# A bank's sigmoid and second product one bank later; the output projection's first two token tiles in two halves over four PSUM banks

## Chip, cores and metric

The kernel runs on one core of one Trainium2 chip. The metric is the device time of one execution in microseconds; lower is better.

## What is computed

A two-layer encoder trunk on 512 tokens of width 1024, all in float32. Per layer (cut to what matters here):

```python
proj = rms_norm(h) @ w_in                       # 1024 -> 9 groups of 512 columns
rq, rk, rv, rg, hq, hf_fwd, hf_bwd, hi, hg = split(proj)
q2 = silu(hq) * 128 ** -0.5                     # HGRN2 query
k  = (1 - lb) * sigmoid(-hf);  f = lb + (1 - lb) * sigmoid(hf)   # two directions; lb = 0 in layer 0
r_out = rms_normalize(retention(rotary(rq), rotary(rk), rv)) * ret_g * silu(rg)
h_out = rms_norm(hgrn2(q2, k, f, hi)) * hgrn_g * silu(hg)
h = h + concat([r_out, h_out]) @ w_out          # 1024 -> 1024
h = h + expert_choice_ffn(rms_norm(h))          # 16 SwiGLU experts, 64 tokens each
```

A final RMSNorm ends it.

## The kernel before, in words

**Order.** `body` runs, for each of the two layers, `mixer` (projections, both recurrences, output projection, router) and then `ffn` (the experts in eight pairs). The program order is written out by hand: every engine takes its instructions in the order in which the Python code emits them, and waits in that order. "Below" names lines of `before.py`.

**Memory.** SBUF has 22 slots of 1 MB, handed out first in, first out by `slot` and returned by `put`. Weights come through one queue, SP's, in the order of `plan` (`pump`, L179). A load into a slot waits until the slot's last reader is done, and the loads behind it wait too. PSUM has eight banks: four with the tag `pj` for the projections and the experts' gate and up products, four with the tag `pb` for all else.

**Precision.** An fp32 product is made of three passes: the operands are split into a high part (fp32r, by ScalarE: L448, L819, L808) and a low part (the rest, by VectorE or GpSimd: L449, L820, L809), and high by high, low by high and high by low are summed in PSUM.

**Projections.** `proj` (L475) makes one group of 512 columns in four banks, one for each 128 columns, in four steps q of 24 matmuls of 128x512; each step takes a quarter of the contraction. In the last step bank c is complete after each six matmuls, and `evacuate(c, ...)` follows at once. The next group takes the same four banks in the same order, so its first matmul into bank c waits for the evacuation of that bank. `split` makes the parts of the step after next's weights and stands in the queues behind the evacuations. The groups run in the order hq, hf_bwd, hf_fwd, hi, rq, rk, rv, rg, hg (n = 0 to 8).

**Evacuations.** `silu_q` (L500 to L502), `forget` (L487 to L493), `gate_out` (L515 to L517) and `mix_out` (L801 to L809) each run all their steps for one bank before the next bank's. VectorE multiplies the bank by the row of 1/rms (`rb`), which frees the bank; ScalarE takes the sigmoid; VectorE waits for it and makes the second product (in `forget` two products with the lower bound, in layer 1 only). In `mix_out` there follow a product with the recurrence's output and the split of the previous bank's result into high and low parts; the last bank's own split comes at its end.

**Side work.** `lead` runs a projection and, each six matmuls, takes some steps of a side generator: in projection 0 `arrive` (transposes of h, their split, the squares, 1/rms, and four small matmuls that spread it over the partitions, L416), in 3 to 7 the recurrences, in 8 `norms` and half of the split of `w_out` (`wout_split`).

**Output projection.** `output` (L925) goes through eight (token tile, half of the columns) pairs. Each takes one `pj` bank, and 24 matmuls: eight contraction tiles k in three passes. k = 0 to 3 are the retention heads, ready during projection 8; k = 4 to 7 are the HGRN2 heads, which `mix_out` delivers at its end. The sum with h (L935), the transposes (L954), the router (L986 to L1017) and the search for each expert's best tokens (L1042) follow as `work`.

**Layer boundary.** The last pair of experts is added to h in column pieces of 512, 256 and 256. The last piece's sums (`last_spread`, L1223 and L1228) are made in layer 1's `arrive`, one bank for each of four token tiles.

## Time and profile before

| | |
|---|---|
| median of three runs | 1668.72 us (1667.14 to 1672.53) |
| the profiled execution | 1667.63 us, of which the span from first to last instruction is 1665.9 us |
| busy PE / VectorE / ScalarE / GpSimd | 1555.7 / 680.3 / 478.4 / 237.4 us |
| mean granted TensorE clock | 0.979 |
| read from HBM | 459.03 MB |

Times in the trace are microseconds from the span's start. PE is TensorE, DVE VectorE, ACT ScalarE, POOL GpSimd; L475 is line 475. In the timeline a line gives start, duration, engine, line, instruction, output and input, the shapes and the count; in square brackets stands the time for which the engine was idle ahead of it, and which instruction released it. The mixer of layer 0 takes the first 385 us, its experts go on to about 835 us; layer 1's mixer ends at about 1208 us.

### The profile page before, as it was taken

The numbers are of one execution on the slowest core, as the hardware profiler recorded it, in microseconds if no ns is written. First come the engines' busy times: TensorE is split into PE (matmuls) and PEld (weight loads), VectorE is DVE, ScalarE is ACT, GpSimd is POOL, SyncE is SP. The second block draws the span as 40 slices with busy tenths as digits, with TensorE's granted clock in tenths as the row PEclk, the third lists the DMA queues.
The fourth block names the chain that finished last, engine by engine and source line by source line (L and its number), as shares of the span: only waits on it lengthen the run. The fifth ranks groups of instructions, "written<-read, shape, count | busy, mean of one in ns | idle before, by whom it ended". The sixth has DMA issues, their size and how long they took to land. (4 is left out here: it accounts for less than half of the span.)

```text
span 1665.9 us, 20044 instructions
## 1 busy us (share of the span) xinstructions
PE 1555.7 (93%) x8020; PEld 965.8 (58%) x8020; DVE 680.3 (41%) x1123; ACT 478.4 (29%) x888; POOL 237.4 (14%) x208
## 2 busy tenths in 40 slices
PE   7989899899999999999999898998899999999986
PEld 6778797675454444433477687976653545444333
DVE  4477955652111312312254889465610213132113
ACT  4444344352130110200243344444422212012003
POOL 1042542200000000011000534421000000000201
PEclk9999999899999999999999899998999999999998
DMA  6120221649999999999950111316689999999997
GB/s 254 53 76 26 76 97 52 250 157 358 426 417 427 426 427 425 427 426 427 401 213 26 51 51 51 122 51 227 268 350 426 424 426 427 427 427 426 426 426 277
DMA packets 94605, 464.53 MB, mean 279 GB/s; under 512 B 7904, under 2 KB 16288, under 8 KB 48432
## 3 DMA queue, kind: packets, MB, share of 16 engines
q1 hardware_dynamic: 93040, 458.35, 67.6%
q0 software_dynamic: 1472, 4.90, 0.8%
q8 instruction: 63, 1.03, 0.2%
q14 instruction: 30, 0.25, 0.0%
HBM read 459.03 MB, written 4.19 MB: 278 GB/s over the span
## 5 line engine op out<-in xcount | busy, mean ns | idle before, releaser
L1168 PE MATMUL pj<-s,s 128*64 128x512 f32 x2048 | 476.1, 596 | 18.0 <-DMA s<-in_w_up_dram 14.7
L475 PE MATMUL pj<-s,s 128*128 128x512 f32 x1728 | 435.6, 405 | 19.7 <-DVE s L449 8.8
L475 PEld LDWEIGHTS pj<-s,s 128*128 128x128 f32 x1728 | 325.6, 193 | 92.2 <-DVE s L449 11.6
L1168 PEld LDWEIGHTS pj<-s,s 128*64 128x64 f32 x2048 | 171.8, 137 | 279.7 <-issue 205.8
L1301 PE MATMUL pb<-s,t 128*64 128x512 f32 x896 | 197.5, 594 | 5.4 <-ACT t L1206 2.7
L1301 PEld LDWEIGHTS pb<-s,t 128*64 128x64 f32 x896 | 65.0, 137 | 127.5 <-issue 113.3
L1085 POOL TENSOR_TENSOR t<-s,t 128x512 fp32r<-128x512 f32 x16 | 20.9, 1327 | 714.8 <-ACT t L1083 714.8
L1216 DVE SCALAR_TENSOR_TENSOR t<-pb,sm,t 128x512 fp32r<-128x512 f32 (+1 forms) x34 | 24.4, 719 | 240.3 <-ACT t L1215 238.8
L1228 DVE TENSOR_TENSOR s<-s,pb 128x512 f32<-128x512 f32 (+1 forms) x116 | 68.7, 653 | 129.7 <-PE pb L1223 129.7
L925 PE MATMUL pj<-s,s 128*128 128x512 f32 x384 | 105.4, 422 | 10.0 <-ACT s L808 6.7
L449 DVE TENSOR_TENSOR s<-s,s 128x1024 fp32r<-128x1024 f32 (+1 forms) x64 | 82.4, 1306 | 28.8 <-ACT s L448 28.5
L925 PEld LDWEIGHTS pj<-s,s 128*128 128x128 f32 x384 | 72.8, 199 | 32.0 <-ACT s L808 9.2
L1133 DVE COPY sm<-pb 128x2 f32<-128x2 f32 x16 | 2.5, 159 | 203.3 <-PE pb L1130 203.3
L1215 ACT ACTIVATE t<-pb,sm 128x512 fp32r<-128x512 f32 (+1 forms) x34 | 22.5, 662 | 194.4 <-PE pb L1301 182.9
L1111 PEld LDWEIGHTS pb<-t,t 128*128 128x128 f32 x512 | 66.0, 203 | 14.0 <-issue 9.7
L448 ACT ACTIVATE s<-s 128x1024 fp32r<-128x1024 f32 (+1 forms) x73 | 73.9, 1035 | 0.1
L1144 ACT ACTIVATE t<-pb 128x512 fp32r<-128x512 f32 x16 | 9.6, 601 | 220.6 <-PE pb L1142 220.6
L1111 PE MATMUL pb<-t,t 128*128 128x256 f32 x512 | 70.5, 296 | 1.6 <-DVE t L1095 0.8
L1223 PE MATMUL pb<-t,t 128*128 128x512 f32 (+1 forms) x264 | 68.0, 398 | 1.0 <-DVE s L1228 0.9
L1223 PEld LDWEIGHTS pb<-t,t 128*128 128x128 f32 x264 | 45.8, 188 | 34.3 <-issue 19.4
L568 DVE TENSOR_TENSOR s<-s,s 128x512 f32<-128x512 f32 x56 | 57.4, 1026 | 13.2 <-PE pb L616 13.2
L1189 ACT ACTIVATE t<-pj,sm 128x512 f32<-128x512 f32 x32 | 22.0, 687 | 140.2 <-PE pj L1168 140.2
(234 smaller groups left out, 1602.7 us busy)
## 6 DMA issues: line engine op xcount, KB each, us to landing
s<-in_w_gate_dram SPq DMA_DIRECT2D x124, 1024.0 KB, 19.5
s<-in_w_up_dram SPq DMA_DIRECT2D x124, 1024.0 KB, 19.5
s<-in_w_down_dram SPq DMA_DIRECT2D x112, 1024.0 KB, 19.5
s<-in_w_in_dram SPq DMA_DIRECT2D x34, 1024.0 KB, 4.8
s<-in_w_down_dram SPq DMA_DIRECT2D x32, 512.0 KB, 10.4
s<-in_w_out_dram SPq DMA_DIRECT2D x8, 1024.0 KB, 4.8
s<-in_x_dram SPq DMA_DIRECT2D x8, 512.0 KB, 3.7
s<-in_w_gate_dram SPq DMA_DIRECT2D x8, 512.0 KB, 11.1
```

What stands on the lines that cost most here:

```text
L448: nc.scalar.activation(wh[:, ks], src[:, ks], AF.Copy)
L449: e.tensor_tensor(low[:, ks], src[:, ks], wh[:, ks], op=OP.subtract)
L475: nc.tensor.matmul(pg[c], lhsT=lhsT, rhs=rhs, start=(k == 0 and m == 0), stop=(k == ND - 1 and m == 2))
L568: v.tensor_tensor(qv, qv, tq, op=OP.mult)
L925: nc.tensor.matmul(po, lhsT=x, rhs=w, start=(k == 0 and i == 0), stop=(k == ND - 1 and i == 2))
L1111: nc.tensor.matmul(pt[:, i], lhsT=x[:, tt, k % 2::2], rhs=oh[:, tt], start=(tt == 0 and x is self.picked[u][0]), stop=(tt == NT - 1 and x ...
L1168: nc.tensor.matmul(pg[n + 2 * f][e * CAP:(e + 1) * CAP], lhsT=self.xe[:, k, at + e * CAP:at + (e + 1) * CAP], rhs=w[e][:, f * 512:(f + 1) ...
L1215: nc.scalar.activation(yH[0][:, cs], py, AF.Copy, scale=gate)
L1216: v.scalar_tensor_tensor(yL[0][:, cs], py, gate, yH[0][:, cs], op0=OP.mult, op1=OP.subtract)
L1223: nc.tensor.matmul(pc, lhsT=ohT[:, tt * P:(tt + 1) * P], rhs=y[:, cs], start=(y is yH[0]), stop=(y is yL[0]))
L1228: v.tensor_tensor(dst, dst, pc, op=OP.add)
L1301: nc.tensor.matmul(py[f][e * CAP:(e + 1) * CAP], lhsT=hT[:, k, e * CAP:(e + 1) * CAP], rhs=W[e][:, k2, f * 512:(f + 1) * 512], start=(k == ...
```

## The change

- `forget`, `silu_q`, `gate_out` and `mix_out` do the product that frees the bank (`scaled`) and the sigmoid at once. The rest is put into a queue (`follow`), which first runs one round of what earlier banks left (`flush(1)`). So a bank's second product stands behind the next bank's first. In `mix_out` the low part lags by one more bank. The last bank's rest is run by `lead` at its second to eleventh step, or by `flush()` at the end of projection 8.
- `output` takes the first two token tiles as four banks: first k = 0 to 3 for all four, then k = 4 to 7. `plan` and `wout_split` take `w_out` with the retention half first.
- `arrive`: 1/rms is spread two steps (twelve matmuls) later; in layer 1 the last piece's squares move ahead of the transposes of k = 4 to 7, and `last_spread` takes two token tiles to a bank.
- The scaling of the rotary table moves from the end of projection 0 to the end of projection 1.
- At the start the gain's transpose stands behind two token tiles, not three; the second half of the first weight's low part goes to GpSimd.

```diff
@@ start
-        self.turn_in(range(4), range(NT - 1))
+        self.turn_in(range(4), range(2))
         self.norm_gain()
-        self.turn_in(range(4), range(NT - 1, NT))
+        self.turn_in(range(4), range(2, NT))
@@ arrive
             self.last_squares(1)
             yield 1.0
+            self.last_squares(2)
...
         for _ in self.rstd_steps(0, NT, self.r):
             yield 1.0
+        yield 1.0
+        yield 1.0
         yield 1.0
@@ split
+                if ks.start:
+                    e = nc.gpsimd
@@ new helpers
+    def scaled(self, dst, ps):
+        self.nc.vector.tensor_tensor(dst, ps, self.rb, op=OP.mult)
+        return dst
+    def follow(self, *steps):
+        self.flush(1)
+        self.second.append(deque(steps))
+    def flush(self, rounds=9):
+        for _ in range(rounds):
+            for d in list(self.second):
+                d.popleft()()
+                if not d:
+                    self.second.remove(d)
@@ forget
-        nc.vector.tensor_tensor(F, ps, self.rb, op=OP.mult)
+        self.scaled(F, ps)
...
-            nc.vector.tensor_scalar(F, F, om, lb, op0=OP.mult, op1=OP.add)
-            nc.vector.tensor_scalar(K, K, om, None, op0=OP.mult)
+            def bound():
+                nc.vector.tensor_scalar(F, F, om, lb, op0=OP.mult, op1=OP.add)
+                nc.vector.tensor_scalar(K, K, om, None, op0=OP.mult)
+            self.follow(bound)
@@ silu_q (gate_out alike)
-        nc.vector.tensor_tensor(q, ps, self.rb, op=OP.mult)
-        nc.scalar.activation(sg, q, AF.Sigmoid)
-        nc.vector.scalar_tensor_tensor(q, q, P ** -0.5, sg, op0=OP.mult, op1=OP.mult)
+        nc.scalar.activation(sg, self.scaled(q, ps), AF.Sigmoid)
+        self.follow(lambda: nc.vector.scalar_tensor_tensor(q, q, P ** -0.5, sg, op0=OP.mult, op1=OP.mult))
@@ mix_out
+        nc.scalar.activation(sg, self.scaled(w, ps), AF.Sigmoid)
+        def mix():
+            v.scalar_tensor_tensor(w, w, g, sg, op0=OP.mult, op1=OP.mult)
+            v.tensor_tensor(o, o, w, op=OP.mult)
+            for H, _, x in self.mixed(NH + c, o):
+                nc.scalar.activation(H, x, AF.Copy)
+        def low():
+            for H, L, x in self.mixed(NH + c, o):
+                v.tensor_tensor(L, x, H, op=OP.subtract)
+        self.follow(mix, low)
@@ lead
+            n += 1
+            if 1 < n < 12:
+                self.flush(1)
@@ output
-        for tt, f in [(tt, f) for tt in range(NT) for f in range(2)]:
+        both, po = [(tt, f) for tt in range(2) for f in range(2)], {}
+        parts = [(tt, f, range(a, a + 4)) for a in (0, 4) for tt, f in both] + \
+            [(tt, f, range(ND)) for tt in range(2, NT) for f in range(2)]
+        for tt, f, ks in parts:
...
+            if ks[-1] < ND - 1:
+                continue
@@ last_spread
-                self.last_spread = lambda: [spread(tt, lo, n) for tt in range(NT)]
+                def last_spread():
+                    for t in range(0, NT, 2):
+                        pc = self.pb().rearrange("p (t c) -> p t c", t=2)
+                        for tt in (t, t + 1):
+                            for y in yH[0], yL[0]:
+                                nc.tensor.matmul(pc[:, tt - t], ...)
+                        h = self.h[t // 2][:, :, lo:]
+                        v.tensor_tensor(h, h, pc, op=OP.add)
```

## The prediction

> **What bounds the kernel now.** I read the slices of the page first, then the table by stage, the chain, and the timeline of the two mixers.

> ```profile
> DMA  6120221649999999999950111316689999999997
> ```
> ```profile
> 500.00:520.00 20.00, 20.00 (x94) 1.00 1.01 426
> ```
> ```profile
> 1607.86 20.83 DMA s<-in_w_up_dram
> ```
> ```profile
> 1158.00:1161.00 3.00, 3.00 (x29) 1.00 0.02 8
> ```

> The slices (41.6 us each) alternate: in both expert stages the DMA engines are full, 426 GB/s in the stage table, and the chain there runs through weight loads of some 20 us each. In the mixers they are nearly empty. So the experts are paced by their weight stream, and the mixers by TensorE and what it waits for. A saving in a mixer reaches the end only if the stream starts earlier by as much. It does: in the output projection the DMA share is 0.02, because all slots are taken; they come free as this projection's tiles and then the first experts' weights are used up, which is tied to TensorE's place. I therefore count every microsecond that a mixer loses less as one microsecond of the end. Next, where TensorE waits.

> **The output projection.** Timeline of layer 1, then the clock there, then layer 0:

> ```profile
> 1122.83 11.08 PE L475 MATMUL pj<-s,s 128*128 128x512 f32 x48
> ...
> 1133.37 0.68 DVE L801 TENSOR_TENSOR t<-pj,s 128x512 f32<-128x512 f32 x1
> ...
> 1134.10 3.02 PE L925 MATMUL pj<-s,s 128*128 128x512 f32 x12 [0.19 <-DVE t L801]
> ...
> 1134.75 0.75 DVE L803 SCALAR_TENSOR_TENSOR t<-t,cols,t 128x512 f32<-128x512 f32 x1 [0.70 <-ACT t L802]
> ...
> 1135.53 0.69 DVE L804 TENSOR_TENSOR s<-s,t 128x512 f32<-128x512 f32 x1
> ...
> 1136.14 0.68 DVE L801 TENSOR_TENSOR t<-pj,s 128x512 f32<-128x512 f32 x1
> ...
> 1137.85 0.73 PE L925 MATMUL pj<-s,s 128*128 128x512 f32 x2 [0.73 <-ACT s L808]
> ...
> 1145.92 1.42 DVE L809 TENSOR_TENSOR s<-s,s 128x256 fp32r<-128x256 f32 x4
> ```
> ```profile
> 1151.15 5.71 PE L925 MATMUL pj<-s,s 128*128 128x512 f32 x24
> ```
> ```profile
> 1143.00:1146.00 3.00, 1.83 (x3) 0.50 0.86 311
> ```
> ```profile
> 310.97 3.01 PE L925 MATMUL pj<-s,s 128*128 128x512 f32 x12 [0.18 <-DVE t L801]
> ...
> 328.24 2.09 PE L925 MATMUL pj<-s,s 128*128 128x512 f32 x8
> ```

> Undisturbed, a matmul costs 11.08 / 48 = 0.231 us. The first pair does its twelve retention matmuls and then waits, head by head, for `mix_out`, whose banks follow each other by about 2.8 us (1133.37, 1136.14); the wait quoted (0.73 us) is the first of a row of them that lasts until the last low part (1145.92 to 1147.34). The granted clock falls to 0.50 on the way. From 1134.10 to 1151.15 TensorE does 30 matmuls (and four transposes, 0.4 us in steady state): 17.05 us for 30 x 0.231 + 0.4 = 7.3 us of work.

> After the change there are 48 retention matmuls to do first, 11.1 us, to about 1145.2. They need a free bank each 2.8 us: VectorE frees the four at 1134.0, 1134.6, 1136.8 and 1139.6 if I lay its queue out with the durations of before (0.68 for a first product, 0.75 + 0.69 for the two behind it, 1.42 / 2 = 0.7 for a low part), so each is in time. The last low part is then due at about 1145.4; the first bank gets to that head after another nine matmuls, at 1147.3. Even with `mix_out` as slow as now (1147.34) the cover holds. Gain 17.05 - 7.3 = 9.8 us in layer 1, and by the same count 328.24 - 310.97 - 7.3 = 10.0 us in layer 0. If only the waits go and the half clock stays, some 2.3 us less (half of a stretch of 3 us, the one quoted, to 6 us), about 7.5 us each. The sums with h come a few matmuls later for tile 0, but both tiles are complete after the same 96 matmuls as before, so router and search keep their places.

> **Projection 0 to 1, layer 0.**

> ```profile
> 44.29 0.68 DVE L500 TENSOR_TENSOR s<-pj,s 128x512 f32<-128x512 f32 x1
> ...
> 46.34 1.22 DVE L847 TENSOR_TENSOR t<-t,s 128x1024 f32<-128x1024 f32 x1
> ...
> 48.26 3.89 ACT L448 ACTIVATE s<-s 128x1024 fp32r<-128x1024 f32 x4
> ...
> 49.35 0.50 PE L475 MATMUL pj<-s,s 128*128 128x512 f32 x1 [2.47 <-ACT s L448]
> ...
> 50.80 50.85 PE L475 MATMUL pj<-s,s 128*128 128x512 f32 x215 [0.95 <-DVE s L449]
> ```
> ```profile
> 52.00:55.00 3.00, 3.00 (x8) 0.50 0.99 354
> ```

> The last bank's first product starts only at 44.29, because each bank waits for the sigmoid of the one before. Behind it stand the rotary table (1.22 us), the lower bound and the next weights' split; TensorE waits 2.47 + 0.95 us and then runs at half clock for some 3 us. With the lag the last first product moves to about 41.6 and the table goes away, so the weights' low part is ready at about 46.7, when TensorE gets there (46.88, the end of its 24 matmuls). 216 matmuls from 46.88 at 0.231 end at 96.8 in place of 101.65: 4.9 us. Bounds: 2.5 (some of the wait and of the slow clock stays) and 5.4.

> **The two starts.**

> ```profile
> 31.52 1.13 PE L416 MATMUL pb<-ident,sm 128*128 128x128 f32 x8 [0.71 <-DVE sm L332]
> ```
> ```profile
> 834.61 0.50 PE L1223 MATMUL pb<-t,t 128*128 128x256 f32 x2 [0.95 <-DVE s L1228]
> ...
> 851.40 1.13 PE L416 MATMUL pb<-ident,sm 128*128 128x128 f32 x8 [1.67 <-DVE sm L332]
> ```

> Twelve more matmuls (2.8 us) ahead of L416 cover its waits of 0.71 and 1.67 us, and 1/rms is still on its way 1.4 us before the first bank is complete. Two banks in place of four take away 0.95 us. Together 0.7 in layer 0 and 2.6 in layer 1 (bounds 1.5 and 2.9). The squares moved ahead on ScalarE delay the split of k = 4 by about 0.6 us, and TensorE needs that only two steps later. The other order at the very start and the half on GpSimd are worth nothing that I can see, 0 to 0.3 us: projection 0 reaches that low part after twenty matmuls.

> **The forget gates, layer 1** (layer 0 has no second product there):

> ```profile
> 867.24 20.56 PE L475 MATMUL pj<-s,s 128*128 128x512 f32 x89 [0.85 <-DVE s L449]
> ...
> 892.58 20.59 PE L475 MATMUL pj<-s,s 128*128 128x512 f32 x89 [0.76 <-DVE s L449]
> ```
> ```profile
> 904.96 0.69 DVE L487 TENSOR_TENSOR s<-pj,s 128x512 f32<-128x512 f32 x1 [9.04 <-PE pj L475]
> ...
> 913.68 0.68 DVE L487 TENSOR_TENSOR s<-pj,s 128x512 f32<-128x512 f32 x1
> ...
> 914.42 1.66 PE L475 MATMUL pj<-s,s 128*128 128x512 f32 x6 [1.25 <-DVE s L487]
> ...
> 915.60 1.04 ACT L448 ACTIVATE s<-s 128x1024 fp32r<-128x1024 f32 x1
> ...
> 916.73 3.27 POOL L449 TENSOR_TENSOR s<-s,s 128x1024 fp32r<-128x1024 f32 x1 [79.77 <-DVE s L493]
> ...
> 920.06 8.00 PE L475 MATMUL pj<-s,s 128*128 128x512 f32 x23 [2.86 <-POOL s L449]
> ```
> ```profile
> 936.96 3.97 PE L475 MATMUL pj<-s,s 128*128 128x512 f32 x12
> ```
> ```profile
> 86.55 0.69 DVE L487 TENSOR_TENSOR s<-pj,s 128x512 f32<-128x512 f32 x1 [10.04 <-PE pj L475]
> ...
> 93.69 2.39 POOL L449 TENSOR_TENSOR s<-s,s 128x1024 fp32r<-128x1024 f32 x1 [48.83 <-ACT s L448]
> ```
> ```profile
> 113.56 3.00 PE L475 MATMUL pj<-s,s 128*128 128x512 f32 x12
> ```

> A bank takes (913.68 - 904.96) / 3 = 2.9 us here and TensorE fills one in 6 x 0.231 = 1.4, so the next group waits for bank 3, and then for its weights, whose split stands behind. With the lag the four first products follow TensorE and end about 4 us earlier. At 0 to 1 the 0.85 us goes. At 1 to 2, 96 matmuls take 25.34 us (867.24 to 892.58) for 22.2: 3.2 us (bounds 2 and 3.3). At 2 to 3 GpSimd's split and the recurrence's first steps on GpSimd and VectorE set the pace afterwards, so I don't take the waits but layer 0 as the measure, where no second product stands in the way: from the first evacuation to the same group of twelve it needs 113.56 - 86.55 = 27.0 us, layer 1 936.96 - 904.96 = 32.0. With about 1 us for the two bounds that stay on VectorE: 4.0 us, bounds 1 and 5.3.

> **The retention gate** (L516 and L517 before the head norms):

> ```profile
> 291.24 0.49 PE L714 MATMUL pb<-t,selR 128*128 128x512 f32 x1 [1.07 <-ACT t L704]
> ```
> ```profile
> 1114.37 0.49 PE L714 MATMUL pb<-t,selR 128*128 128x512 f32 x1 [1.78 <-ACT t L704]
> ```

> The sigmoids end about 1.5 us earlier, but the last bank's product (0.75 us) now falls into the chain of the norms. I take 0.3 and 1.0 us, bounds -0.8 and 1.8 for each.

> **Sum.** Layer 0: 0.7 + 4.9 + 0.3 + 10.0 = 15.9. Layer 1: 2.6 + 0.9 + 3.2 + 4.0 + 1.0 + 9.8 = 21.5. Together 37.4 us: 1667.63 - 37.4 = 1630.2 us, by the profiled execution, which lies 1.1 us under the median of the three runs. I put the forecast at 1630.5.

> **Rivals.** *The lag does little.* Only the four banks and the starts work (19.8 + 3.3), since behind each bank some other queue is due at once. For it: at 920.06 the wait names GpSimd. Against it: the wait of 2.47 us at 49.35 goes back to VectorE's order. About 1644.5; chance 0.07.

> *Four banks cost the clock.* The 48 matmuls go through four banks; if that kept the granted clock at 0.50 in both layers, they would take 11.1 us more each: 1652.7. Against it stands 1122.83: the projections go through four banks too, at 0.231. Chance 0.02. [...]

> *The stream hides it.* If the experts' loads were fixed by something other than TensorE's place, the mixers' gain would be waited away: 1667.6, no change. Against it stands the empty DMA at 1158. Chance 0.03.

> *VectorE and GpSimd get in each other's way, and it is slower.* The same GpSimd split takes 2.39 us at 93.69 and 3.27 us at 916.73, where VectorE works beside it: 0.9 us more. The change lays 64 lagged VectorE instructions (24 in layer 0, 40 in layer 1) beside GpSimd's splits and recurrence steps. If each cost 0.9 us on the path, 58 us against 37: about 1688. It decides from 42 of them on; most lie where GpSimd is idle. Chance 0.02. [...]

> *It does not do what it says*: `flush` would have to stand ahead of the next bank's first product in VectorE's queue. In the diff `scaled` comes first everywhere, so I leave that inside the first rival.

> **Chances.** Forecast 0.86, the rivals as given. Faster by over 0.3% (5 us, about what can be told here) 0.95, the same 0.03, slower 0.02. The range: the lower bounds of the terms add up to some 21 us, the upper ones to 41; with the first rival inside and a few microseconds for a stage that runs on at full clock, 1622 to 1646.

> **What would show it.** Right: L925 in one run of 48 matmuls of about 11 us in each layer with no wait for L808 or L809; granted clock 1.00 there; no wait of L475 for L487; projection 1 of layer 0 without a wait for the weights' split; no wait ahead of L416. The mixers 16 and 21 us shorter, the expert stages as long as now. Wrong: waits in the second half of the four banks, expert stages that grow by what the mixers lose, or longer GpSimd instructions at the recurrence's start.

## The result and the profile after

The changed kernel takes 1630.76 us (median of four runs, 1630.17 to 1632.15), the kernel before 1667.93 us beside it (four runs, 1666.37 to 1672.53): a ratio of 0.9774, interval 0.9753 to 0.9795. The profiled execution took 1630.17 us (span 1628.4, mean granted clock 0.986), 37.46 us less than the one of before.

TensorE's way through the two mixers, in spans between first matmuls of a kind, in us:

| stretch | layer 0 before | after | layer 1 before | after |
|---|---|---|---|---|
| start of the span or of the expert stage to first projection matmul | 12.85 | 11.26 | 442.03 | 441.01 |
| projections 0 to 2, to the recurrence's first parity sum | 89.09 | 84.13 | 96.57 | 82.88 |
| parity sums, to the first level (L616, now L640) | 10.49 | 10.33 | 7.54 | 10.51 |
| to the first head norm row (L714, now L738) | 178.81 | 178.22 | 178.94 | 178.86 |
| to the first output matmul (L925, now L961) | 19.73 | 19.72 | 19.73 | 19.73 |
| output projection and router, to the first gather (L1111, now L1149) | 74.64 | 65.13 | 74.11 | 65.12 |
| to the first expert matmul | 3.68 | 3.39 | 3.44 | 3.54 |
| last experts, to the end | | | 454.25 | 454.57 |

The rows add up to the span. Up to its first expert, layer 0 is 17.1 us shorter, layer 1's mixer 19.7, the first expert stage 1.0, and the last expert stage is 0.3 longer: 37.5 us less. So what TensorE no longer waits for reaches the end, and the expert stages keep their length. The page after, its DMA slices and the table by stage for one of them:

```profile
DMA  6121121668999999999950121217799999999997
```
```profile
500.00:520.00 20.00, 19.85 (x106) 10.15 (x104) 5.46 (x9) 2.57 (x4) 0.00 (x0) 1.00 1.01 426
```

The full slices are as many as before and the stream runs at the same 426 GB/s. That it begins earlier shows in the table: layer 0's first expert matmul stands at 372.18 us in place of 389.29.

**Output projection.** Timeline of TensorE, layer 0 and layer 1 of the kernel after, and VectorE beside layer 1:

```profile
303.66 14.59 PE L961 MATMUL pj<-s,s 128*128 128x512 f32 x63 [0.19 <-DVE t L489]
...
1105.17 14.57 PE L961 MATMUL pj<-s,s 128*128 128x512 f32 x63 [0.18 <-DVE t L489]
...
1104.44 1.27 DVE L489 TENSOR_TENSOR t<-pj,s 128x512 f32<-128x512 f32 x2
...
1107.21 0.68 DVE L489 TENSOR_TENSOR t<-pj,s 128x512 f32<-128x512 f32 x1
...
1109.87 0.68 DVE L489 TENSOR_TENSOR t<-pj,s 128x512 f32<-128x512 f32 x1
...
1115.73 0.76 DVE L835 TENSOR_TENSOR s<-s,s 128x256 fp32r<-128x256 f32 x2 [0.48 <-ACT s L831]
```

The 63 matmuls of the first two token tiles up to the first transpose run without a wait, 14.57 / 63 = 0.231 us each. The four banks come free 0.1 us before the first output matmul (the second 0.5, the third 2.7 and the fourth 5.4 after it), and the last low part (L835) ends 11.3 us after it. The first bank gets to that head only after 57 matmuls, 13.2 us. The table of windows for that stretch of layer 1, before and after:

```profile
1134.00:1151.00 17.00, 12.09 (x33) 7.55 (x34) 10.99 (x21) 5.81 (x14) 0.00 (x0) 0.70 0.94 337
```
```profile
1105.17:1119.74 14.57, 14.57 (x63) 11.75 (x63) 10.75 (x20) 5.25 (x12) 0.00 (x0) 1.00 0.98 338
```

In the first row TensorE does 33 matmuls (30 of the output, the rest transposes) in 17 us at a mean clock of 0.70, in the second 63 in 14.6 us at 1.00. VectorE does 21 and 20 instructions of nearly the same total (10.99 and 10.75 us): it is no faster, only in another order.

**Projections, layer 0 and layer 1.** TensorE's timeline of the kernel after:

```profile
32.18 1.05 PE L418 MATMUL pb<-ident,sm 128*128 128x128 f32 x8
...
45.90 49.20 PE L479 MATMUL pj<-s,s 128*128 128x512 f32 x215 [0.90 <-DVE s L453]
...
832.97 1.05 PE L418 MATMUL pb<-ident,sm 128*128 128x128 f32 x8
833.78 54.91 PE L479 MATMUL pj<-s,s 128*128 128x512 f32 x241
890.27 5.51 PE L479 MATMUL pj<-s,s 128*128 128x512 f32 x23 [1.59 <-POOL s L453]
896.07 0.73 PE L627 MATMUL pb<-s,parity 128*128 128x512 f32 x2 [0.28 <-ACT s L618]
899.16 0.73 PE L627 MATMUL pb<-s,parity 128*128 128x512 f32 x2 [2.35 <-POOL s L619]
...
902.57 2.50 PE L479 MATMUL pj<-s,s 128*128 128x512 f32 x5 [2.46 <-DVE s L453]
```

The last row's counterpart before:

```profile
931.10 1.45 PE L475 MATMUL pj<-s,s 128*128 128x512 f32 x5 [0.22 <-DVE s L449]
```

The spread of 1/rms (L418) waits for nothing. In layer 0 the wait of 2.47 us for ScalarE is gone and 0.90 of the 0.95 us for the low part is left. In layer 1 one run of 241 matmuls (0.228 us each) stands where before six waits cut it, and of the wait of 2.86 us for GpSimd's split 1.59 is left. Then come the parity sums, where TensorE waits for GpSimd (L619, 2.35 us) and for a low part of VectorE (2.46 us, before 0.22): this stretch of layer 1 is 3.0 us longer than before (the last section).

**Head norms.** The kernel after, the row before the norms and their first row:

```profile
1070.62 8.49 PE L479 MATMUL pj<-s,s 128*128 128x512 f32 x29 [1.79 <-DVE s L453]
...
1085.44 0.49 PE L738 MATMUL pb<-t,selR 128*128 128x512 f32 x1 [0.79 <-ACT t L728]
```

The wait at the norms fell from 1.78 to 0.79 us. The row above it took 8.49 us for its 29 matmuls; what that means follows below.

### The profile page after: what moved, and what is told of

Same layout as the page of the kernel before. It is cut to its first block, busy times and chain, and to the rows that moved or that the text cites. A ratio compares the mean times of both kernels' runs of the same rounds, so it can differ in the third digit from the quotient of the medians.

```text
span 1628.4 us, 20039 instructions
## 1 busy us (share of the span) xinstructions
PE 1543.3 (95%) x8020; PEld 960.0 (59%) x8020; DVE 675.3 (41%) x1120; ACT 478.2 (29%) x888; POOL 237.5 (15%) x209
## 5 line engine op out<-in xcount | busy, mean ns | idle before, releaser
L479 PE MATMUL pj<-s,s 128*128 128x512 f32 x1728 | 432.7, 403 | 11.3 <-DVE s L453 8.9
L453 DVE TENSOR_TENSOR s<-s,s 128x1024 fp32r<-128x1024 f32 (+1 forms) x63 | 84.2, 1351 | 35.9 <-ACT s L450 35.7
L961 PE MATMUL pj<-s,s 128*128 128x512 f32 x384 | 95.1, 398 | 0.4 <-DVE t L489 0.4
L961 PEld LDWEIGHTS pj<-s,s 128*128 128x128 f32 x384 | 69.8, 189 | 15.9 <-DVE t L489 1.2
L1149 PEld LDWEIGHTS pb<-t,t 128*128 128x128 f32 x512 | 65.9, 203 | 14.2 <-issue 9.7
L1149 PE MATMUL pb<-t,t 128*128 128x256 f32 x512 | 70.3, 296 | 2.1 <-DVE t L1133 1.3
```

Of the source, the lines that this page charges most:

```text
L453: e.tensor_tensor(low[:, ks], src[:, ks], wh[:, ks], op=OP.subtract)
L479: nc.tensor.matmul(pg[c], lhsT=lhsT, rhs=rhs, start=(k == 0 and m == 0), stop=(k == ND - 1 and m == 2))
L961: nc.tensor.matmul(po[tt, f], lhsT=x, rhs=w, start=(k == 0 and i == 0), stop=(k == ND - 1 and i == 2))
L1149: nc.tensor.matmul(pt[:, i], lhsT=x[:, tt, k % 2::2], rhs=oh[:, tt], start=(tt == 0 and x is self.picked[u][0]), stop=(tt == NT - 1 and x ...
```

## The experiments

Each kernel ran on a chip beside the kernel before, which took 1667.6 to 1667.9 us there.

My theory: TensorE's waits behind `mix_out`, `forget`, `silu_q` and 1/rms are the whole loss, and each is a matter of order alone; every microsecond of them, with the half clock that follows, reaches the end. Rivals: the lag is worth little and the banks do it all, or the other way about; the experts' stream hides part; the clock falls for another reason than the waits.

**e1: the four banks alone.** The kernel before with the `output` loop, the order of `plan` and `wout_split` of the change.

> The kernel before, with only the output projection's four banks and the order of w_out that goes with them; all evacuations stay as before. My theory: the 48 retention matmuls (11.1 us) cover mix_out even without its lag, because its last low part ends 13.2 us after the first L925 (1134.10 to 1147.34) and the first bank gets there after 57 matmuls, 13.2 us. So each layer's output stage is about 9 us shorter, as in the changed kernel (62.7 to 53.7 us from the first L925 to the last tile's first router group in layer 1), and the time is 1667.9 - 18 = 1650. A rival: the cover needs the lag too; then waits for L809 stand in the second half of the four banks and the gain is 13 us or less, 1655.

Measured: 1654.01 us, ratio 0.9915 (0.9901 to 0.993), so 13.6 us gained and 23.2 left to the rest. The rival "the lag does little" falls. It was to be 1650, though: the output projection became 7.7 and 8.2 us shorter, not 9 each. The time is nearer to the rival's 1655, but no wait for L809 stands in the second half. TensorE and VectorE in layer 1 of this kernel:

```profile
1136.88 0.76 DVE L809 TENSOR_TENSOR s<-s,s 128x256 fp32r<-128x256 f32 x2
1137.55 0.69 DVE L801 TENSOR_TENSOR t<-pj,s 128x512 f32<-128x512 f32 x1
...
1138.29 6.41 PE L929 MATMUL pj<-s,s 128*128 128x512 f32 x27 [0.50 <-DVE t L801]
```

The bank's first product (L801) stands behind all of the bank before, its low part (L809) last. Banks come free 3.5 us apart (1134.04, 1137.55), and TensorE takes 12 x 0.231 = 2.8 us for a bank's half: it waits for the fourth bank, in layer 0 for the third (0.43 us) and the fourth (0.45). The other part is not this edit's: this execution needed 106.0 us from layer 1's first projection matmul to its first level, the one of before 104.1, and then 20.94 us from the head norms to the first output matmul in place of 19.73. Nothing there was edited (the last section has what the runs showed of such differences).

**e2: all of the change without the banks.** The changed kernel with the three pieces of e1 put back.

> The changed kernel with the output projection and the order of w_out put back; the lag, the starts and the table's move stay. My theory: mix_out's heads now follow each other by 2.65 us in place of 3.5, so the first pair's waits come to about 6 us per layer, and the clock falls again for another 1 to 2 us: 1630.8 + 14 to 17 = 1645 to 1648. If the gain of the banks does not depend on the lag at all, 1630.8 + 18 = 1649. The rival that the lag does little and the banks do all: 1630.8 + 18 + 14 would be wrong here, since nearly the whole 37 us should be gone: 1660 or more.

Measured: 1645.22 us, ratio 0.9863 (0.9848 to 0.9878): 14.5 us slower than the change, as expected. e1's and e2's gains (13.6 and 22.3 to 22.7) add up to 35.9 to 36.3 of the 37.2. Here TensorE does fifteen matmuls of the output and then waits for each head, layer 0:

```profile
306.91 0.98 PE L957 MATMUL pj<-s,s 128*128 128x512 f32 x3 [1.56 <-ACT s L831]
309.57 0.96 PE L957 MATMUL pj<-s,s 128*128 128x512 f32 x3 [1.68 <-ACT s L831]
312.20 4.21 PE L957 MATMUL pj<-s,s 128*128 128x512 f32 x9 [1.67 <-ACT s L831]
```

A lagged `mix_out` alone shortens this stage by 1.5 and 2.3 us (73.13 and 71.85 us to the first gather). The lag sets how fast heads come; only the banks give TensorE something else to do until then.

**e3: the forget gates' bounds at once.**

```diff
-            self.follow(bound)
+            bound()
```

> The changed kernel with the forget gates' products with the lower bound at once again, not one bank later; layer 0 is untouched by it. My theory: in layer 1 the boundaries of projections 1 to 2 and 2 to 3 get their waits back, 3.2 and 4.0 us: 1630.8 + 7 = 1638, all of it between the first forget evacuation of layer 1 and the recurrence's first level. The rival: the GpSimd split and the recurrence behind it set the pace there anyway, so 3 us or less, 1633.

Measured: 1639.25 us (1635.14 to 1641.34), ratio 0.9818 (0.9801 to 0.9836), 8.5 us slower than the change. TensorE and VectorE of this kernel, layer 1:

```profile
867.64 1.64 PE L479 MATMUL pj<-s,s 128*128 128x512 f32 x6 [1.24 <-DVE s L489]
869.81 1.22 DVE L884 TENSOR_TENSOR t<-t,s 128x1024 f32<-128x1024 f32 x1
869.91 0.50 PE L479 MATMUL pj<-s,s 128*128 128x512 f32 x1 [0.64 <-ACT s L450]
872.22 22.18 PE L479 MATMUL pj<-s,s 128*128 128x512 f32 x89 [1.80 <-DVE s L453]
```

The wait for the fourth bank's evacuation is back with its two followers, twice in the layer. The forecast gave these two boundaries 3.2 + 4.0 = 7.2 us. The 8.5 measured are not the lag alone: the rotary table (L884), which the change moved to the end of projection 1, now stands ahead of the weights' low part, and the wait for that is 1.80 us, before 0.76; the 89 matmuls behind it took 22.18 us, before 20.59. The 0.9 us that the forecast gave to the boundary of projections 0 to 1 is not in this experiment: no wait stands there.

**e4: the query's and the gate's second products at once.** The two `self.follow(lambda: ...)` of `silu_q` and `gate_out` run their product on the spot.

> The changed kernel with silu_q's and gate_out's second products at once again. My theory: layer 0 loses 2 to 4 us at the boundary of projections 0 to 1 (the rotary table stays out of the way, so less than the 4.4 that came from both), layer 1 up to 0.9 there, and the retention gate 1 us per layer in the wait of the head norms: 1630.8 + 4 to 7 = 1635 to 1638. The rival: the lag does nothing at these two places and the table's move did it all at the first: 1631.

Measured: 1633.15 us, ratio 0.9793 (0.9779 to 0.9808), 2.4 us slower than the change, less than expected, and its interval overlaps with the change's. From 1/rms to the first parity sum layer 0 needs 66.09 us in place of 63.21, with the wait of 1.51 us for ScalarE's split back; in layer 1 the projections take 84.60 us in place of 82.88. At the norms the wait is 1.81 us again, but the stretch up to them is no longer (177.64 us, in the change 178.86): this execution did the 29 matmuls ahead of it at full clock.

**e5: the rotary table at the end of projection 0 again.**

> The changed kernel with the rotary table scaled at the end of projection 0 again. My theory: its 1.22 us on VectorE stand ahead of the next weights' low part, so layer 0's wait at the boundary of projections 0 to 1 grows from 0.90 to about 2.1 us, and the granted clock may fall after it for another 1.5 us; in layer 1 nothing: 1632 to 1634. A rival: the table is made while ScalarE loads its table and the lower bound waits, and nothing changes.

One run: 1630.59 us. I expected 1632 to 1634; the move is worth nothing that shows, as the rival had it. TensorE's wait, layer 0 of this kernel:

```profile
45.04 15.26 PE L479 MATMUL pj<-s,s 128*128 128x512 f32 x66 [0.95 <-DVE s L453]
```

0.95 us against the 0.90 of the change. ScalarE and VectorE of the change show what the low part waits for without the table:

```profile
41.94 1.28 ACT L270 ACT_TABLE_LOAD   x1
...
43.35 3.89 ACT L450 ACTIVATE s<-s 128x1024 fp32r<-128x1024 f32 x4
43.48 0.16 DVE L271 TENSOR_TENSOR lbwork<-lbwork 128x4 f32<-128x4 f32 x1 [0.98 <-ACT lbwork L270]
...
44.63 1.22 DVE L453 TENSOR_TENSOR s<-s,s 128x1024 fp32r<-128x1024 f32 x1
```

ScalarE loads a table of its own for the lower bound's exponential (1.28 us) and makes it before the weights' high part. VectorE waits 0.98 us for the exponential, finishes the bound and only then makes the low part. The rotary table of 1.22 us fell for the most part into that wait.

**e6: the two starts as before.** The edits of `start`, `arrive`, `split` and `last_spread` undone.

> The changed kernel with all edits at the two layers' starts undone: order of the transposes and the half on GpSimd, place of 1/rms, place of the last squares, one bank for each token tile in the last sums. My theory: 0.6 us in layer 0 (the wait ahead of L416 is back) and 2.6 us in layer 1: 1630.8 + 3.2 = 1634. The first matmul of projection 0 came 1.6 us earlier in the changed kernel, with the second x tile in place at 6.5 and not at 8.4 us; I put that down to the transfer and not to the edit. If it is the edit, the tile lands at about 8.4 here.

One run: 1634.42 us, 3.7 us over the change. The waits of layer 1 are back (0.95 and 1.65 us), and the projections there take 86.01 us in place of 82.88: the starts are worth 3.1 us in layer 1. In layer 0 the first projection matmul stands at 12.40 us in place of 11.26, and projections 0 to 2 take 83.63 us, not longer than the 84.13 of the change.

**e11: the half on GpSimd alone undone** (`if ks.start: e = nc.gpsimd` left out of `split`).

> The changed kernel with the second half of the first weight's low part on VectorE again; nothing else. In four kernels with the old start the second x tile was in place at 7.9 to 8.4 us, in six with the new one at 6.4 to 6.9. My theory now: the GpSimd instruction stands ahead of the constants' transfers in GpSimd's queue, which go out at 13.0 us in place of 1.25, and so leave the DMA engines to x; then the tile lands at about 8 us here, and projection 0 starts at 12.4 to 12.8 in place of 11.3. The rival: the order of the transposes does it; then it lands at 6.4 to 6.9 here.

One run: 1630.58 us. The time tells nothing, because a half clock of 1.6 us that the change's trace has in layer 0 (29 matmuls in 8.47 us) did not come in this one (6.91 us). The start itself tells it. GpSimd and VectorE at the start, the change first, then this kernel:

```profile
6.48 0.69 DVE L300 SCALAR_TENSOR_TENSOR t<-s 128x512 bf16<-128x512 f32 x1 [1.50 <-DMA s<-in_x_dram]
...
11.81 1.29 POOL L453 TENSOR_TENSOR s<-s,s 128x512 fp32r<-128x512 f32 x1 [11.37 <-ACT s L450]
13.03 0.72 POOL L240 DMA_DIRECT2D t<-in_lmask_dram  x1
```
```profile
1.25 0.70 POOL L240 DMA_DIRECT2D t<-in_lmask_dram  x1 [0.81 <-POOLq L1431]
...
8.39 0.69 DVE L300 SCALAR_TENSOR_TENSOR t<-s 128x512 bf16<-128x512 f32 x1 [3.52 <-DMA s<-in_x_dram]
```

With the half on GpSimd, the split stands in GpSimd's queue ahead of the issue of the constants (L240), which so go out at 13.03 us and not at 1.25; the second tile of x is there at 6.48 in place of 8.39, and the first projection matmul starts at 11.26 in place of 12.88. From 4 to 6 us the DMA engines move 306 and 352 GB/s in the change, and 212 and 186 here, where the constants' transfers run beside those of x, as in the kernel before (228 and 192, L240 at 1.25 us). In e6's expectation I had blamed the transfer and not the edit; that was wrong.

**e7: the waits of before filled.** The kernel before, with six matmuls into a spare bank, whose result nobody reads, ahead of each HGRN2 head of the first pair. It takes away no wait for `mix_out`; it only keeps TensorE at work.

```diff
+                if tt == f == 0 and 3 <= k < 7:
+                    fill = self.pb()
+                    for _ in range(6):
+                        nc.tensor.matmul(fill, ...)
```

> The kernel before, with 24 extra matmuls per layer, whose results nobody reads, put into the waits of the output projection's first pair (six, 1.4 us, behind each of k = 3 to 6). They take no wait away. If the granted clock falls there because TensorE does too little in a stretch, it now stays at 1.00 and each layer gains the part of the loss that was half clock, 1.5 to 2.3 us: 1667.9 - 4 = 1664. If it falls for another reason, the extra matmuls gain nothing or cost up to 5.5 us per layer.

Measured: 1668.48 us, ratio 1.0 (0.9991 to 1.001). In time it missed. In the table of windows it hit, the half-clock window of before and its counterpart here:

```profile
1143.00:1146.00 3.00, 1.83 (x3) 0.50 0.86 311
```
```profile
1143.00:1146.00 3.00, 2.19 (x9) 1.00 0.95 276
```

With the added matmuls the clock is 1.00 over the whole stretch (1134 to 1158), and the stage is 0.9 and 1.4 us shorter (73.75 and 72.68 us), though it does 24 more matmuls. So the half clock there came from how little TensorE had to do. Why the whole is no shorter is only known for this one execution: in layer 1 the parity sums take 9.26 us in place of 7.54, and the way from the head norms to the first output matmul 20.96 in place of 19.73, in lines that were not edited. For the other nine it stays open.

**e8 to e10: what is left on the engines.** e8 moves one low part of projection 3's weights from GpSimd to VectorE (the wait of 1.59 us at 890.27); e9 gives the four steps of `wout_split` a cost of 4.4, so that they spread over projection 7 (the wait of 1.79 us at 1070.62); e10 does both.

```diff
-            e = nc.gpsimd if self.GROUPS[i // 4] in (7, 2) and i % 2 or ...
+            e = nc.gpsimd if self.GROUPS[i // 4] in (7, 2) and i % 2 and i != 13 or ...
...
-                yield next(wo)
+                next(wo)
+                yield self.WO_COST
```

What was expected, in this order:

> The changed kernel with one low part of the weights of projection 3 (the one TensorE waits for, 1.59 us, ahead of the recurrence) on VectorE in place of GpSimd, where it took 3.83 us in layer 1 beside VectorE and 2.39 in layer 0. If GpSimd's queue sets the recurrence's start, its first sums (L604) come 2 to 4 us earlier per layer and everything behind them: 1630.8 - 4 to 8 = 1623 to 1627. If VectorE's own queue sets it, its extra 1.2 us take the gain back: 1630.

> The changed kernel with the first four steps of w_out's split in projection 7 spread out, one for every second step of the projection, not all four at once. In the changed kernel the next weights' low part stands behind two of them on VectorE (5.93 us beside GpSimd's 5.75) and TensorE waits 1.79 us in each layer, after which the granted clock was at 0.50 to 0.58 for some 3 us. My theory: the wait goes in both layers, and the half clock with it: 1630.8 - 4 to 7 = 1624 to 1627. The rival: the split is only moved, and the head norms or mix_out wait for it instead: 1630 or more.

> The spread-out split of w_out and the low part on VectorE together, on the changed kernel. If the two gains are independent: 3.4 us, which the second alone measured, and 4 to 7 us from the first: 1620 to 1624. If the first gives nothing: 1627.

Measured: e8 1627.36 us (ratio 0.9753, 0.9737 to 0.9769), e9 1626.08 (0.9747, 0.9734 to 0.9761), e10 1624.21 (0.9732, 0.9719 to 0.9745): 3.4, 4.7 and 6.6 us under the change, though only e10's interval lies below the change's own. e9 hit its expectation, e8 and e10 missed theirs by 0.4 and 0.2 us. Where e8's gain comes from is not shown: its parity sums start 0.5 and 1.3 us earlier, counted from the first projection matmul, not 2 to 4. In e9 the same 29 matmuls as above:

```profile
1067.91 6.89 PE L480 MATMUL pj<-s,s 128*128 128x512 f32 x29 [0.68 <-DVE s L454]
```

The wait fell from 1.79 to 0.68 us, and the matmuls behind it took 6.87 and 6.89 us in the two layers, against 8.47 and 8.49.

**e12: e10 with the recurrence's start filled.** Eight matmuls with no reader stand ahead of the third parity sum.

```diff
+                if c == i - 2 == 0:
+                    fill = self.pb()
+                    for _ in range(8):
+                        nc.tensor.matmul(fill, ...)
```

> The same as the two edits together, and eight extra matmuls per layer, whose results nobody reads, between the high and the low half of the recurrence's first sums, where TensorE waits for GpSimd. They take no wait away. Where extra matmuls filled the waits of the output projection, the clock stayed at 1.00. If that holds here, the five matmuls and the sums behind them (2.50 and 1.9 us at half clock in the changed kernel) run at full clock, 1.5 to 2 us less in each layer: 3 us under the kernel with the two edits. If the second wait, which stays empty (2.4 us), is enough to lower it, the same time or 0.5 us more.

Measured: 1618.47 us (1617.82 to 1622.77), ratio 0.9709 (0.9693 to 0.9724): under the kernel before and the change; against e10 the intervals just overlap. From the first projection matmul to the first level layer 1 takes 90.17 us in place of e10's 92.09. The table of windows over the recurrence's start, e10 and e12:

```profile
889.00:911.00 22.00, 16.37 (x67) 12.82 (x66) 19.86 (x18) 7.24 (x13) 13.94 (x9) 0.84 0.14 48
```
```profile
889.00:911.00 22.00, 19.18 (x95) 15.21 (x96) 19.62 (x20) 9.06 (x18) 15.17 (x10) 1.00 0.29 96
```

The clock stays at 1.00. But VectorE and GpSimd also took turns in another order here (the last section), so how much of the 5.7 us is the clock and how much the order is not separated.

## Why the prediction was right, step by step

- **Output projection** (9.8 and 10.0): 9.5 in layer 0 and 9.0 in layer 1. The order of VectorE's queue that I laid out came true to 0.1 us: the last low part due 11.3 us after the first output matmul, measured 11.3. One sentence failed: "even with `mix_out` as slow as now the cover holds". I had held only the last low part against it. e1 shows that the earlier limit is the freeing of the banks, 3.5 us each against 2.8.
- **Projection 0 to 1, layer 0** (4.9) and **the starts, layer 0** (0.7): together 5.0 on the path from the first projection matmul to the parity sums, not 5.6. 0.90 us of the wait stays, though projection 1 was to have none. Two steps failed. I had the rotary table on the path; e5 shows that ScalarE's exponential and the bound behind it are. And "1/rms is still on its way 1.4 us before the first bank": the weights' split stands between. ScalarE, VectorE after:

```profile
33.27 0.60 ACT L422 ACTIVATE s<-pb 128x512 f32<-128x512 f32 x1 [5.01 <-PE pb L418]
...
34.84 1.23 DVE L453 TENSOR_TENSOR s<-s,s 128x1024 fp32r<-128x1024 f32 x1 [4.65 <-ACT s L450]
35.99 1.28 DVE L489 TENSOR_TENSOR s<-pj,s 128x512 f32<-128x512 f32 x2
```

  1/rms is there at 33.87, but VectorE first makes a low part whose high part came behind 1/rms on ScalarE, so the first product starts at 35.99, when the second bank is waiting too (the count is x2).
- **The very start** (0 to 0.3): 1.6 us. It was mis-sized, because I looked at VectorE and TensorE only and not at what else stands in GpSimd's queue (e11).
- **Starts and forget gates, layer 1** (2.6 + 0.9 + 3.2 + 4.0 = 10.7): 10.7 from the first projection matmul to the first level (104.11 to 93.39), but not in the places named. The projections alone became 13.7 us shorter, and the parity sums 3.0 longer. e6 (3.1 for 2.6) and e3 (8.5 for 7.2, the rotary table's wait among it) confirm the single terms within some 1.3 us. That the whole came out to a tenth is luck, since it holds the parity sums, which differ by 1.7 to 1.8 us between executions of unchanged lines (7.54 us before, 9.33 in e1, 9.26 in e7).
- **Retention gate** (0.3 and 1.0): the waits at the norms fell by 0.25 and 0.99 us, as said. The stretch became 0.6 us shorter in layer 0 and 0.1 in layer 1. In layer 1 the gain went into a half clock behind a wait that both kernels have: 29 matmuls took 6.91 us before and 8.49 after. In e4, without this lag, the same wait was followed by 6.87 us.
- **The rest**: 1.0 us in the first expert stage and 0.3 at the edge of layer 0's search were not forecast; the last expert stage gave back 0.3.
- **The rivals.** "The lag does little": e1 and e3 speak against it. "Four banks cost the clock": 1.00 over all 63 matmuls in both layers. "The stream hides it": the expert stages kept their length to 1 us. "VectorE and GpSimd get in each other's way": GpSimd's split at the recurrence's start took 3.83 us in place of 3.27 in layer 1, 0.6 us, and 2.39 as before in layer 0. Beside it stands the order of two engines at the parity sums (the last section), which came out both ways with the code of before.

Taken away one at a time, banks (14.5), forget bounds (8.5), query and gate (2.4) and starts (3.7) make 29.1 us of 37.2. e3's part holds the rotary table's wait, and the starts rest on one run. The rest is the lag in `mix_out` and what the parts gain together; I have not split it further. In the output stage that lag takes off 1.5 and 2.3 us without the four banks (e2), and with them 1.8 and 0.8 (66.91 and 65.87 us in e1, 65.13 and 65.12 in the change).

## What to carry to other kernels

Where an evacuation makes a round trip through a second engine, write the instruction that frees the next bank ahead of the one that waits for the trip, and check the freeing of every bank against the consumer's pace, not only the last result. Where a consumer waits for late operands, look for the half of its sum whose operands are ready and give it as many banks as the wait is long. Before counting an instruction as free on an idle engine, read that engine's whole queue: its DMA issues move with it (here from 1.25 to 13.03 us).

## What the runs showed of the hardware

**Half clock after short waits: it depends on where they fall.** In both layers of before, of the change and of e11, and in layer 1 of e4, TensorE waits 1.78 to 1.82 us for a low part ahead of the same 29 matmuls. In four of these seven places the 29 then took 8.46 to 8.49 us, in three 6.87 to 6.91. Before, layer 1, without; its table of windows for TensorE alone (busy time, count, granted clock), and the one of the change around the wait at 1070.62, with half clock:

```profile
1100.14 6.91 PE L475 MATMUL pj<-s,s 128*128 128x512 f32 x29 [1.79 <-DVE s L449]
```
```profile
1096.06:1099.47 3.41, 2.29 (x11) 1.00 0.00 0
1099.47:1102.89 3.42, 2.75 (x12) 1.00 0.00 0
```
```profile
1068.07:1071.48 3.41, 1.62 (x8) 1.00 0.00 0
1071.48:1074.90 3.42, 3.42 (x10) 0.50 0.00 0
```

A fall behind this wait costs 1.6 us and, in these two traces, goes with where the wait falls on the grid, so the gain from such a wait taken away is uncertain by that much. Behind the shorter wait of 0.68 us, in layer 1 of e9 and in both layers of e12, the 29 took 6.87 to 6.89 us.

**Who goes first costs some 2 us.** GpSimd's two low parts and one of VectorE's meet at the recurrence's start (L619 and L453 after). GpSimd and VectorE of e10, then of e12:

```profile
893.33 5.29 POOL L620 TENSOR_TENSOR s<-s,s 128x1024 fp32r<-128x1024 f32 x2 [9.27 <-ACT s L619]
...
896.28 3.43 DVE L454 TENSOR_TENSOR s<-s,s 128x1024 fp32r<-128x1024 f32 x1 [2.07 <-ACT s L451]
```
```profile
889.43 6.44 POOL L620 TENSOR_TENSOR s<-s,s 128x1024 fp32r<-128x1024 f32 x2 [9.26 <-ACT s L619]
...
892.40 1.23 DVE L454 TENSOR_TENSOR s<-s,s 128x1024 fp32r<-128x1024 f32 x1 [2.07 <-ACT s L451]
```

Either VectorE takes 3.43 us and GpSimd 5.29, or VectorE 1.23 and GpSimd 6.44. Of GpSimd's two, the second takes 2.34 us in the first case and 3.47 in the second. 1.23 and 2.34 make 3.57, near the 3.43 and 3.47 of the slowed one: it looks as if the one that comes second waits for the other. That is my estimate from these sums; no trace shows what it would wait for. Of the nine such meetings in before, the change, e11 and e12 (two each) and layer 1 of e10 VectorE came first in three: layer 1 of before, and both layers of e12. The parity sums took 7.5 us there in before and 7.9 and 8.6 in e12, and 9.3 to 10.5 elsewhere; in e12 the added matmuls and the full clock may have a part in it. VectorE starts 2.95 to 3.00 us after GpSimd's first in both outcomes, so what decides is not seen in the trace. With the same code there, e1 and e7 needed 1.9 and 2.0 us more than before from layer 1's first projection matmul to its first level.
